# One more group of four FFN tiles with a seven-product down projection, and an end ordered by token tiles

## The chip, the cores and the metric

The kernel runs on one core of a Trainium2 chip. The metric is the device time of the core in microseconds (us). Lower is better.

## The reference

One layer of a decoder trunk over 512 tokens of width 1024, in float32. A combined input projection feeds a block-sparse attention group, an SSD (Mamba-2) group and a pooling group; their concatenation is projected and added to x. Then follows what the change touches, a SwiGLU FFN of hidden width 2816, and a final RMSNorm:

```
h = rmsnorm(x, norm_ffn)
gate, up = split(h @ w_gate_up, 2)
x = x + (silu(gate) * up) @ w_down
out = rmsnorm(x, norm_final)
```

## The kernel before

Every float32 product is made of three matmuls (`mm3`): both operands are split into a high part rounded to fp32r and a low remainder, and high x high, high x low and low x high are summed in a PSUM bank. A split costs one ScalarE copy and one VectorE subtraction (`hi_lo`).

**Tiles.** The FFN's hidden width is cut into 22 tiles of 128. For tile i, gate and up over two halves of the tokens and two halves of the width form a 2x2 by 2x2 block product, made by seven products instead of eight (`block(i, n)`, n from 1 to 7, each of 12 matmuls of 256 columns). Products 1, 6, 7 and 4 accumulate in the left half of one bank (B); after 1, 6 and 7 ScalarE copies the running sum out (`u<-psB`, line 1275). Products 2 (A) and 5, 3 (C) go to another. `block_out` makes the activation from them, with high priority.

**Weights.** Raw weights come by DMA from SP into four buffers of the tag `raw` (`r_g`, `r_u` for gate and up, `r_d`, `r_r` for the down projection), are split into the rings `w` (8 tiles) and `wx` (10), and are used. Sums of weights that the seven products need come in two ways. From tile `ADD_FROM` on, the host's array `wgs` is loaded by SP and a second part is added on the way by a DMA from POOL (`sa`, `sum_ahead`), with two VectorE additions left (lines 1001 and 1002). Tiles before it do four additions on VectorE (lines 1009 to 1012) and load the up weights whole. `sum_ahead` is first called in tile `ADD_FROM - 1` and then once for each later tile.

**Down projection.** `GROUPS` orders the tiles into groups. A group in `FAST` has four tiles and a down projection of seven products, again over two halves of the tokens, of the output columns and of the hidden rows (`down_step`, named by product 1 to 7 and half a or b; each has two token tiles of 128, three matmuls of 512 columns each). Its operands are made by `out_fast` and `split_r`, two of its weight sums come by accumulating DMA (`sar`), two by VectorE (lines 1054 and 1055). Its steps are merged into the first two tiles of the next group by the list `MERGED`, in which n0, n1 and nl are that group's first and second tile and the tile before it. Product results are added to or subtracted from `x1`, the residual, by VectorE. A group that is not in `FAST` has a plain down projection: for both column halves h, tiles k and four token tiles t, one `mm3` of 512 columns (banks `pd`).

**The end.** In the last group (18 to 21) h = 1 runs by token tile (banks `pdl`): after the four tiles' matmuls of one token tile VectorE adds the bank to x1, ScalarE squares with a running sum, `last_rstd` makes the reciprocal root (ScalarE's square root, then four small VectorE operations), and the two halves of the row are scaled, one on VectorE and one on ScalarE (`left_out`), and sent out. The last token tile is split in two parts of 256 columns (`LAST`).

**Order.** The program order is a list (`steps`) written from these tables; `advance` places the next weight split as soon as its ring has room and a clock estimate says that the data is there. A scheduler then orders the instructions of each engine by its own estimate of readiness and by priority. `tc.issue_after(x)` forces an instruction behind x. Each engine serves its instructions in the order that results.

## Time and profile before

| | |
|---|---|
| median of 3 runs | 560.72 us (559.87 to 560.85) |
| profiled execution | 560.42 us |
| its span | 558.70 us |
| TensorE busy | 98% of the span, 3464 matmuls |
| VectorE busy | 81% |
| ScalarE busy | 57% |
| DMA | 80.51 MB, 144 GB/s on average |

PE is TensorE, PEld its weight loads, DVE is VectorE, ACT ScalarE, POOL GpSimd; SPq, ACTq and POOLq are the queues that issue DMAs. A busy share is over the span. Idle time is put down to the instruction that released the engine.

### The profile page before, as it was taken

Reading aid. Unit: us, or ns where it says so; the run is one execution under the profiler, and the core shown is the slowest. Engines: PE = TensorE matmul, PEld = TensorE weight load, DVE = VectorE, ACT = ScalarE, POOL = GpSimd, SP = SyncE. Lnnn points to the kernel's source line nnn. Section 1 sums busy time; section 2 is a strip of 40 time slices with the busy share of each in tenths; the row PEclk is TensorE's granted clock in tenths of the full one; section 3 lists DMA queues with packets and bytes.
Section 4 is the critical chain, followed back from the end, with each engine's and each line's share of the span. In section 5 each row is a group of like instructions: output and inputs, shape, how many; then the busy total and the mean of one; then the engine's idle time right before and its main releaser. Section 6 shows DMA issues by size and latency. Waiting matters only on the chain.

```text
span 558.7 us, 9204 instructions
## 1 busy us (share of the span) xinstructions
PE 546.7 (98%) x3464; PEld 495.1 (89%) x3464; DVE 450.8 (81%) x832; ACT 316.3 (57%) x589; POOL 51.2 (9%) x73
## 2 busy tenths in 40 slices
PE   8999999999999999999899999999999999999995
PEld 4998998888887889998799999899999998999984
DVE  6489766898998777997768898989899797966456
ACT  6676635777678547554345555555655545434344
POOL 2020002006110001001101110101110010000000
PEclk9999999999999999999999999999999999999999
DMA  8952232423213602389736577856975575622004
GB/s 285 310 172 77 76 129 99 132 77 97 73 39 116 262 1 57 96 260 261 213 95 172 138 196 189 251 134 189 208 220 145 156 216 149 170 76 76 1 2 150
DMA packets 29312, 80.51 MB, mean 144 GB/s; under 512 B 3388, under 2 KB 5076, under 8 KB 29268
## 3 DMA queue, kind: packets, MB, share of 16 engines
q1 hardware_dynamic: 24372, 66.29, 35.4%
q0 software_dynamic: 4320, 12.58, 13.4%
q10 hardware_dynamic: 576, 1.05, 0.5%
q8 instruction: 27, 0.44, 0.3%
q14 instruction: 17, 0.14, 0.1%
HBM read 77.80 MB, written 2.11 MB: 143 GB/s over the span
## 4 chain that ended last, share of the span: by engine, by line
PE 80%; DVE 11%; DMA 4%; ACT 2%; issue 1%; SPq 1%; DVEq 0%; ACTq 0%
PE psB L201 6%; PE psB L200 6%; PE psB L199 6%; PE psA L201 5%; PE psA L200 5%; PE psA L199 5%; PE pc L199 4%; PE pc L201 4%; PE pc L200 4%; PE po L199 2%; PE po L200 2%; PE po L201 2%; PE pn L199 2%; PE pn L200 2%; PE pn L201 2%; PE dnB L199 2%
## 5 line engine op out<-in xcount | busy, mean ns | idle before, releaser
L1275 ACT COPY u<-psB 128x256 f32<-128x256 f32 x63 | 23.0, 366 | 46.9 <-PE psB L201 46.6
L169 DVE TENSOR_TENSOR wlo<-raw,whi 128x1024 fp32r<-128x1024 f32 (+4 forms) x35 | 37.2, 1065 | 12.4 <-ACT whi L168 9.2
L168 ACT ACTIVATE whi<-raw 128x1024 fp32r<-128x1024 f32 (+4 forms) x36 | 31.9, 890 | 21.9 <-PE pc L200 11.6
L199 PE MATMUL pc<-hT_hi,whi 128*128 128x512 f32 x104 | 41.7, 401 | 0.0
L201 PE MATMUL pc<-hT_hi,wlo 128*128 128x512 f32 x104 | 40.8, 392 | 0.0
L200 PE MATMUL pc<-hT_lo,whi 128*128 128x512 f32 x104 | 40.7, 391 | 0.0
L927 DVE TENSOR_TENSOR gl<-r_g,gh 128x1024 fp32r<-128x1024 f32 x22 | 26.8, 1218 | 9.5 <-ACT gh L926 9.5
L986 POOL DMA_DIRECT2D sa<-wgs x18 | 15.6, 869 | 184.9 <-DMA sa<-wgs 49.4
L926 ACT ACTIVATE gh<-r_g 128x1024 fp32r<-128x1024 f32 x22 | 23.2, 1054 | 13.7 <-DMA r_g<-wgu 7.5
L927 DVE TENSOR_TENSOR sl<-sa,sh 128x1024 fp32r<-128x1024 f32 x21 | 25.6, 1217 | 3.3 <-ACT sh L926 3.3
L926 ACT ACTIVATE sh<-r_g 128x1024 fp32r<-128x1024 f32 x18 | 19.0, 1057 | 15.8 <-PE psA L200 6.4
L199 PE MATMUL pd<-dh,aTh 128*128 128x512 f32 x64 | 24.8, 395 | 1.7 <-DVE g L1267 1.5
L199 PE MATMUL po<-whi,mixT_hi 128*128 128x512 f32 x64 | 25.5, 400 | 0.0
L926 ACT ACTIVATE sh<-sa 128x1024 fp32r<-128x1024 f32 x21 | 22.2, 1056 | 5.6 <-PE psB L200 4.2
L200 PE MATMUL po<-wlo,mixT_hi 128*128 128x512 f32 x64 | 25.0, 390 | 0.0
L201 PE MATMUL psB<-T2h,sl 128*128 128x256 f32 x84 | 24.0, 285 | 0.9 <-DVE sl L927 0.9
L200 PE MATMUL pd<-dl,aTh 128*128 128x512 f32 x64 | 24.7, 392 | 0.0
L926 ACT ACTIVATE vh<-r_u 128x512 fp32r<-128x512 f32 x21 | 13.2, 630 | 20.3 <-DMA r_u<-wgu 11.7
L927 DVE TENSOR_TENSOR sl<-r_g,sh 128x1024 fp32r<-128x1024 f32 x18 | 21.9, 1218 | 3.1 <-ACT sh L926 3.1
L199 PE MATMUL psB<-T2h,sh 128*128 128x256 f32 x84 | 23.8, 284 | 0.0
L199 PE MATMUL psB<-h_hi,gh 128*128 128x256 f32 x84 | 23.8, 284 | 0.0
L200 PE MATMUL psA<-h_lo,gh 128*128 128x256 f32 x84 | 23.8, 283 | 0.0
(393 smaller groups left out, 2026.6 us busy)
## 6 DMA issues: line engine op xcount, KB each, us to landing
r_g<-wgu SPq DMA_DIRECT2D x22, 512.0 KB, 4.3
sa<-wgs SPq DMA_DIRECT2D x18, 512.0 KB, 4.5
sa<-wgs POOLq DMA_DIRECT2D x18, 512.0 KB, 6.7
raw<-w SPq DMA_DIRECT2D x13, 512.0 KB, 3.2
r_d<-wd SPq DMA_DIRECT2D x10, 512.0 KB, 4.0
r_u<-wgu SPq DMA_DIRECT2D x18, 256.0 KB, 3.9
r_r<-wd SPq DMA_DIRECT2D x18, 256.0 KB, 3.2
raw<-wo SPq DMA_DIRECT2D x8, 512.0 KB, 3.2
```

The source lines that it names most:

```text
L168: high = nc.scalar.activation(hi[:, sl], raw[:, sl], AF.Copy)
L169: eng.tensor_tensor(lo[:, sl], raw[:, sl], hi[:, sl].bitcast(F32), ALU.subtract)
L199: nc.tensor.matmul(ps, s_hi, m_hi, start=first, stop=False, skip_group_check=chain)
L200: nc.tensor.matmul(ps, s_hi, m_lo, start=False, stop=False, skip_group_check=chain)
L201: last_mm = nc.tensor.matmul(ps, s_lo, m_hi, start=False, stop=last, skip_group_check=chain)
L926: high[name] = nc.scalar.activation(hi, src, AF.Copy).ins
L927: eng.tensor_tensor(lo, src, hi.bitcast(F32), ALU.subtract)
L986: nc.gpsimd.dma_start(t_, wgs[2 * key[0] + 1], accum_op=ALU.add)
L1275: nc.scalar.copy(u_, e["B"])
```

## The change

The fifth group becomes tiles 16 to 19 and joins `FAST`; the last group is tiles 20 and 21. The fifth group's seven products are merged into tiles 20 and 21 by a list of their own, `ENDING`. In it product 5 has banks of its own (D), and product 2's banks are left open: the last two tiles' plain down projection, the steps `k` (k, which tile or 2 for both, token tile, column half), is added onto them for token tiles 0 and 1 of the left half. Product 3 is done inside the steps k220 and k230, onto D for token tile 2 and into a new bank for token tile 3, whose x1 takes D's content by an addition of its own. From product 3 of tile 21 on, `at_end` forces TensorE's order step by step. Token tiles now finish one after the other: `half_done` squares the first half and multiplies it by the final norm's weights, `finish` does what followed the last half. `ADD_FROM` goes from 4 to 5, so tile 4 adds its weights on VectorE. The diff, cut:

```diff
-GROUPS = ((0, 4), (4, 8), (8, 12), (12, 16), (16, 18), (18, 22))
+GROUPS = ((0, 4), (4, 8), (8, 12), (12, 16), (16, 20), (20, 22))
 NA = 4
 NRAW = 4
-FAST = (1, 2, 3)
+FAST = (1, 2, 3, 4)
...
+ENDING = (
+    "n0.1 1a nl.4 n0.2 1b nl.3 2a n0.5 6a n0.6 2b n0.7 6b n1.1 n0.4 7a n1.2 7b n0.3 n1.5 4a n1.6 4b n1.7 n1.4 n1.3 5a 5b k000 k001 k100 k101 k010 k011 k110 k111 k021 k121 k031 k131 k220 k230"
+).split()
-ADD_FROM = 4
+ADD_FROM = 5
...
         def left_out(t, r, queue=nc.scalar):
-            nc.scalar.activation(x1[t][:, :512], x1[t][:, :512], AF.Copy, scale=r)
-            queue.dma_start(out[t * P : (t + 1) * P, :512], x1[t][:, :512])
+            cs = slice(0, 512) if t < 2 else slice(512, 1024)
+            nc.scalar.activation(x1[t][:, cs], x1[t][:, cs], AF.Copy, scale=r)
+            queue.dma_start(out[t * P : (t + 1) * P, cs], x1[t][:, cs])
 
         def last_rstd(t):
 
             y = tiny.tile([P, 1], F32, name=f"rsfy{t}", tag="rsy")
             v = tiny.tile([P, 1], F32, name=f"rsfv{t}", tag="rsv")
             a = tiny.tile([P, 1], F32, name=f"rsfa{t}", tag="rsa")
-            root[t] = nc.scalar.activation(y, ss[:, t, 1:2], AF.Sqrt, scale=1.0 / D, bias=ss[:, t, 0:1]).ins
-            nc.vector.scalar_tensor_tensor(v, ss[:, t, 1:2], -0.5 / D, sh[:, t : t + 1], ALU.mult, ALU.add)
+            root[t] = nc.scalar.activation(y, ss[:, t, 1:2], AF.Sqrt, bias=ss[:, t, 0:1]).ins
+            nc.vector.tensor_scalar(v, ss[:, t, 1:2], ss[:, t, 0:1], -0.5, ALU.add, ALU.mult)
...
-                for m in MERGED:
+                for m in ENDING if hi_ == FT else MERGED:
                     if m[0] == "n":
                         put((base[m[:2]], int(m[3])))
+                    elif m[0] == "k":
+                        put(("k", *map(int, m[1:])))
                     else:
                         put(("r", gi - 1, int(m[0]), "ab".index(m[1])))
-            tiles = [i for i in range(lo_, hi_) if i not in PLAIN]
+            tiles = [i for i in range(lo_, hi_) if i not in PLAIN] if hi_ < FT else []
             for i, nxt in zip(tiles, tiles[1:] + [None]):
                 put(*((i, n) for n in ((1, 2, 5, 6, 7) if i >= ADD_FROM else (1, 2, 6, 5, 7))))
-                if nxt is None and hi_ == 18:
-                    put((hi_, 1), (i, 4), (hi_, 2), (i, 3))
-                elif nxt is None:
+                if nxt is None:
 
                     tail = [] if gi in FAST else [(i, 4), (i, 3)]
...
+                    elif q[0] == "k":
+                        if q[1] > 1:
+                            want((R_RING[2], 2, split_r, GROUPS[gi - 1][0] // 2, 3))
+                        want(("w", 2, split_d, lo_ // 2, q[3]))
...
-            if gi not in FAST:
+            if gi == 0 and gi not in FAST:
...
-                mm3(ps, w_hi[:, sl], w_lo[:, sl], *moving(n, kt), new and kt == 0, kt == 3, chain=not new)
+                mm_ = mm3(ps, w_hi[:, sl], w_lo[:, sl], *moving(n, kt), new and kt == 0, kt == 3, chain=not new)
+            if (i, n) == (FT - 1, 3):
+                at_end.append(mm_)
...
+        at_end, scaled = [], []
+        def behind(*ins):
+            return tc.issue_after(*ins) if ins else nullcontext()
 
         def down_step(_, gi, n, c):
 
             kp0 = GROUPS[gi][0] // 2
             w_hi, w_lo = need(("r", kp0, n))
-            which = "B" if n in (1, 6, 7, 4) else "A"
+            ending = GROUPS[gi][1] == FT - 2
+            which = "B" if n in (1, 6, 7, 4) else "D" if ending and n == 5 else "A"
             if (gi, which) not in acc:
                 acc[gi, which] = [bank(f"dn{which}{v}_{gi}") for v in range(2)]
             ps = acc[gi, which]
             js = slice(c * 512, (c + 1) * 512)
             a_hi, a_lo = aT[n, kp0 + c]
             new = n in (1, 2, 5)
+            goes_on = ending and n == 2
             for v in range(2):
                 vs = slice(v * P, (v + 1) * P)
-                mm3(ps[v], a_hi[:, vs], a_lo[:, vs], w_hi[:, js], w_lo[:, js], new and c == 0, c == 1, chain=not new)
+                with behind(*at_end):
+                    mm_ = mm3(ps[v], a_hi[:, vs], a_lo[:, vs], w_hi[:, js], w_lo[:, js], new and c == 0, c == 1, chain=not new)
+                if at_end:
+                    at_end[0] = mm_
             if c:
                 done(R_RING[n - 1], 2)
                 ops.pop(("r", kp0, n))
@@ -1411,9 +1430,84 @@
                         x_ = x1[t0 + v][:, cs]
                         if op:
                             nc.vector.tensor_tensor(x_, x_, ps[v], ALU.subtract)
-                        else:
+                        elif not goes_on:
                             add(x_, ps[v], x_)
+                        if ending and n == 5 and v == 1:
+                            add_x1(3, 0, ps[v])
+                if ending and n == 7:
+                    gf[0] = x1p.tile([P, D], F32, name="gf", tag="gn")
+                    nc.sync.dma_start(gf[0], gfin.to_broadcast([P, D]))
             advance()
+        def sq_out(t, c):
+            return rawp.tile([P, 1024], F32, name=f"sqf{t}{c}", tag="raw")
+        def half_done(t, h):
+            cs = slice(h * 512, (h + 1) * 512)
+            sq = nc.scalar.activation(sq_out(t, 0)[:, :512], x1[t][:, cs], AF.Square, scale=D**-0.5, accum_out=ss[:, t, 0:1])
+            if t == NT - 1:
+                with tc.issue_after(sq.ins):
+                    left_out(1, rs[1])
+            nc.vector.tensor_scalar_add(ss[:, t, 0:1], ss[:, t, 0:1], EPS)
+            nc.vector.tensor_tensor(x1[t][:, cs], x1[t][:, cs], gf[0][:, cs], ALU.mult)
+        def finish(t, h):
+            with behind(*scaled):
+                r = last_rstd(t)
+            if t in (1, 3):
+                with tc.issue_after(root[t]):
+                    left_out(t - 1, rs[t - 1], nc.sync if t == NT - 1 else nc.scalar)
+            rs[t] = r
+            os_ = slice(h * 512, (h + 1) * 512)
+            scaled[:] = [nc.vector.scalar_tensor_tensor(x1[t][:, os_], x1[t][:, os_], r, gf[0][:, os_], ALU.mult, ALU.mult).ins]
+            nc.sync.dma_start(out[t * P : (t + 1) * P, os_], x1[t][:, os_])
+            if t == NT - 1:
+                left_out(t, r)
+        banks_k = {}
+        def last_step(_, j, t, h):
+            kp, gi = FT // 2 - 1, len(GROUPS) - 2
+            w_ = need(("d", kp, h))
+            ts_ = slice(t * P, (t + 1) * P)
+            work = [(aT[FT - 2 + j_][0][:, ts_], aT[FT - 2 + j_][1][:, ts_], w_, j_) for j_ in ((j,) if j < 2 else range(2))]
+            if j > 1:
+                k3 = GROUPS[gi][0] // 2
+                w3, vs = need(("r", k3, 3)), slice((t - 2) * P, (t - 1) * P)
+                work = [(aT[3, k3 + c][0][:, vs], aT[3, k3 + c][1][:, vs], w3, c) for c in range(2)] + work
+            goes_on = h == 0 and t < 3
+            for part in (slice(0, 512),) if (t, h) != (NT - 1, 0) else (slice(0, LAST), slice(LAST, 512)):
+                key = (t, h, part.start)
+                if key not in banks_k:
+                    banks_k[key] = acc[gi, "D" if t > 1 else "A"][t % 2] if goes_on else bank(f"k{t}{h}{part.start}")
+                ps = banks_k[key]
+                for n, (a_hi, a_lo, w, c) in enumerate(work):
+                    js = slice(c * 512 + part.start, c * 512 + part.stop)
+                    with behind(*at_end):
+                        mm_ = mm3(ps[:, part], a_hi, a_lo, w[0][:, js], w[1][:, js], not goes_on and j != 1 and n == 0, j > 0 and n == len(work) - 1, chain=goes_on)
+                    at_end[0] = mm_
+                if j == 0:
+                    continue
+                x_ = x1[t][:, h * 512 + part.start : h * 512 + part.stop]
+                with tc.high_priority():
+                    add_ = nc.vector.tensor_tensor(x_, ps[:, part], x_, ALU.add)
+                    if (h == 0) == (t < 2):
+                        half_done(t, h)
+                        continue
+                    more = part.stop < 512
+                    nc.scalar.activation(sq_out(t, 1 + more)[:, part], x_, AF.Square, scale=D**-0.5, accum_out=ss3 if more else ss[:, t, 1:2])
+                    if more:
+                        continue
+                    if part.start:
+                        with tc.issue_after(add_.ins):
+                            nc.vector.tensor_tensor(ss[:, t, 0:1], ss3, ss[:, t, 0:1], ALU.add)
+                    finish(t, h)
 
...
+                elif q[0] == "k":
+                    last_step(*q)
...
-            if gi in FAST:
+            if gi or gi in FAST:
...
-                    for t in range(NT):
-                        add_x1(t, h, pss[t])
-                        if gi == len(GROUPS) - 1:
-                            if t == 0:
-                                gf[0] = x1p.tile([P, D], F32, name="gf", tag="gn")
-                                nc.sync.dma_start(gf[0], gfin.to_broadcast([P, D]))
-                            square(t, h, rawp)
-                            nc.vector.tensor_scalar_mul(sh[:, t : t + 1], ss[:, t, 0:1], -0.5)
-                            nc.vector.tensor_tensor(x1[t][:, :512], x1[t][:, :512], gf[0][:, :512], ALU.mult)
...
-                        parts = (slice(0, 512),) if t < NT - 1 else (slice(0, LAST), slice(LAST, 512))
-                        for part in parts:
-                            ps = bank(f"pdl_{t}_{part.start}")
-                            for k in range(lo_, hi_):
-                                w_hi, w_lo = ops["d", k // 2, h]
-                                js = slice((k % 2) * 512 + part.start, (k % 2) * 512 + part.stop)
-                                with tc.issue_after(pd_end):
-                                    pd_end = mm3(ps[:, part], aT[k][0][:, ts_], aT[k][1][:, ts_], w_hi[:, js], w_lo[:, js], k == lo_, k == hi_ - 1)
...
```

## Rows read from the trace of the kernel before

**Rows 1.** The page: span, busy time and share of each engine.

```profile
span 558.7 us, 9204 instructions
...
PE 546.7 (98%) x3464; PEld 495.1 (89%) x3464; DVE 450.8 (81%) x832; ACT 316.3 (57%) x589; POOL 51.2 (9%) x73
```

**Rows 2.** Busy time by stretch: from and to in us, its length, busy us of PE, PEld, DVE, ACT and POOL (instructions), granted TensorE clock, DMA share, GB/s.

```profile
200.00:300.00 100.00, 97.59 (x689) 91.11 (x687) 79.55 (x133) 51.89 (x91) 8.00 (x9) 1.00 0.53 146
300.00:520.00 220.00, 220.00 (x1564) 207.31 (x1563) 192.09 (x300) 116.40 (x191) 18.35 (x21) 1.00 0.63 167
350.00:450.00 100.00, 100.00 (x708) 94.11 (x707) 92.88 (x147) 55.28 (x91) 11.38 (x13) 1.00 0.71 189
450.00:550.00 100.00, 99.74 (x657) 91.36 (x657) 71.12 (x123) 44.48 (x79) 1.73 (x2) 1.00 0.31 88
550.00:558.70 8.70, 2.02 (x17) 1.82 (x16) 4.23 (x16) 4.09 (x11) 0.00 (x0) 0.90 0.61 226
```

**Rows 3.** TensorE's timeline where it was idle (start, us, instruction, idle time before it and what ended it); the last of these rows is also the first matmul that uses tile 21.

```profile
233.40 0.38 PE L201 MATMUL psB<-T2h,sl 128*128 128x256 f32 x1 [0.47 <-DVE sl L927]
...
238.69 0.39 PE L201 MATMUL psB<-T2h,sl 128*128 128x256 f32 x1 [0.44 <-DVE sl L927]
...
269.54 0.50 PE L199 MATMUL pd<-dh,aTh 128*128 128x512 f32 x1 [1.48 <-DVE g L1267]
...
537.94 0.50 PE L199 MATMUL pd<-dh,aTh 128*128 128x512 f32 x1 [0.26 <-ACT aTh L926]
```

**Rows 4.** TensorE's timeline: the end of the first group's down projection; the last matmul of tile 21's product 7, the first of twelve wide matmuls, the first of twenty-four narrow ones (products 4 and 3), and the first wide one behind them.

```profile
279.25 0.28 PE L199 MATMUL psB<-h_hi,gh 128*128 128x256 f32 x1
...
529.03 0.28 PE L201 MATMUL psB<-T3h,sl 128*128 128x256 f32 x1
529.15 0.40 PE L199 MATMUL pd<-dh,aTh 128*128 128x512 f32 x1
...
531.90 0.28 PE L199 MATMUL psB<-T4h,vh 128*128 128x256 f32 x1
...
534.77 0.40 PE L199 MATMUL pd<-dh,aTh 128*128 128x512 f32 x1
```

**Rows 5.** VectorE's groups from 350 to 450 us: line, operation, shapes, count | busy us, mean ns | idle before.

```profile
L927 DVE TENSOR_TENSOR rl<-r_r,rh 128x1024 fp32r<-128x1024 f32 x8 | 9.7, 1218 | 4.2 <-PE psB L200 4.2
...
L927 DVE TENSOR_TENSOR a2l<-a,a2h 128x512 fp32r<-128x512 f32 x3 | 2.0, 681 | 0.0
...
L927 DVE TENSOR_TENSOR a1l<-a,a1h 128x256 fp32r<-128x256 f32 x3 | 1.3, 418 | 0.0
```

**Rows 6.** The same for ScalarE.

```profile
L926 ACT ACTIVATE rh<-r_r 128x1024 fp32r<-128x1024 f32 x8 | 8.5, 1059 | 2.5 <-DMA r_r<-wd 1.2 <-PE psA L200 1.1 <-PE dnB L201 0.2
```

**Rows 7.** Timeline of ScalarE and VectorE between tile 21's product 7 and the use of its activation.

```profile
529.40 0.37 ACT L1275 COPY u<-psB 128x256 f32<-128x256 f32 x1 [1.69 <-PE psB L201]
529.81 0.43 DVE L1267 TENSOR_TENSOR psB<-psA,u 128x256 f32<-128x256 f32 x1 [0.81 <-ACT u L1275]
...
535.86 1.28 ACT L1289 ACT_TABLE_LOAD   x1
...
537.27 0.61 ACT L926 ACTIVATE aTh<-a 128x512 fp32r<-128x512 f32 x1
...
537.92 0.69 DVE L927 TENSOR_TENSOR aTl<-a,aTh 128x512 fp32r<-128x512 f32 x1 [1.61 <-ACT aTh L926]
```

**Rows 8.** Around the wait at 269.5 us: from the chain that ended last (start, us, what), SP's timeline, VectorE's, and times from issue to landing (KB each, us): of the 225 to 300 us stretch for `sa`, of the whole run for `r_g`.

```profile
249.05 7.71 DMA r_g<-wgu
...
261.26 4.36 DMA r_u<-wgu
...
269.15 0.34 DVE g L1267
...
245.85 1.46 SPq L985 DMA_DIRECT2D sa<-wgs  x2
...
259.95 0.68 DVE L1001 TENSOR_TENSOR r_g<-sa,r_g 128x512 f32<-128x512 f32 x1
...
sa<-wgs SPq DMA_DIRECT2D x5, 512.0 KB, 5.7
sa<-wgs POOLq DMA_DIRECT2D x5, 512.0 KB, 6.7
...
r_g<-wgu SPq DMA_DIRECT2D x22, 512.0 KB, 4.3
```

**Rows 9.** VectorE's timeline at the end, and the last output's issue.

```profile
540.34 2.48 DVE L825 TENSOR_TENSOR x<-pd,x 128x512 f32<-128x512 f32 x4 [1.73 <-PE pd L201]
...
547.08 0.15 DVE L865 SCALAR_TENSOR_TENSOR rsfv<-ss,sh 128x1 f32<-128x1 f32 x1
...
548.03 0.75 DVE L1514 SCALAR_TENSOR_TENSOR x<-x,rsfy,gf 128x512 f32<-128x512 f32 x1
548.69 0.16 DVE L866 RECIPROCAL rsfy<-rsfy 128x1 f32<-128x1 f32 x1
...
552.06 0.42 DVE L1498 TENSOR_TENSOR x<-pdl,x 128x256 f32<-128x256 f32 x1 [0.49 <-PE pdl L201]
...
552.66 0.74 DVE L1514 SCALAR_TENSOR_TENSOR x<-x,rsfy,gf 128x512 f32<-128x512 f32 x1
...
554.92 0.33 SPq L1515 DMA_DIRECT2D out<-x  x1
```

More of the change, by code (lines that the diff above doesn't have):

```diff
@@ L12 @@
-from contextlib import ExitStack
+from contextlib import ExitStack, nullcontext
 import numpy as np
@@ L815, in layer @@
         ss3 = x1p.tile([P, 1], F32, name="ss3")
-        sh = x1p.tile([P, NT], F32, name="sh")
         wxp = fpool("wx", 10)
@@ L828, in square @@
             cs = slice(h * 512, (h + 1) * 512)
-            if p_ is rawp:
-                j_ = rawp.tile([P, 1024], F32, name=f"sqf{t}{h}", tag="raw")[:, :512]
-            else:
-                j_ = p_.tile([P, 512], BF16, name=f"sq{t}{h}", tag="sq", bufs=1)
+            j_ = p_.tile([P, 512], BF16, name=f"sq{t}{h}", tag="sq", bufs=1)
             nc.scalar.activation(j_, x1[t][:, cs], AF.Square, accum_out=ss[:, t, h : h + 1])
@@ L1413, in down_step @@
                             nc.vector.tensor_tensor(x_, x_, ps[v], ALU.subtract)
-                        else:
+                        elif not goes_on:
                             add(x_, ps[v], x_)
-            advance()
+                        if ending and n == 5 and v == 1:
[3 more added lines that the diff above has]
+                    nc.sync.dma_start(gf[0], gfin.to_broadcast([P, D]))
@@ new lines, in layer @@
+                pss = [bank(f"pd{gi}{h}_{t}") for t in range(NT)]
+                for kp in range(lo_ // 2, hi_ // 2):
+                    w_hi, w_lo = need(("d", kp, h))
+                    for j in range(2):
+                        k = 2 * kp + j
+                        js = slice(j * 512, (j + 1) * 512)
+                        if h == 0 and k == lo_ + 1:
+                            for q in tail:
+                                block(*q)
+                        for t in range(NT):
+                            ts_ = slice(t * P, (t + 1) * P)
+                            mm3(pss[t], aT[k][0][:, ts_], aT[k][1][:, ts_], w_hi[:, js], w_lo[:, js], k == lo_, k == hi_ - 1)
+                        advance()
+                    done("w", 2)
+                    advance()
@@ L1518, in layer @@
+                for t in range(NT):
+                    add_x1(t, h, pss[t])
+                    advance()
         fctx.close()
```

46 lines of the change are left out of this document (removed).

## The prediction

> **What bounds the kernel now.** I read the page first, then the busy time by stretch, then TensorE's waits, then its timeline. TensorE is busy 98% of the span and VectorE 81% [rows 1]. The stretches say more: from 300 us to 520 us TensorE is busy in every microsecond, at full granted clock; between 200 and 300 us and at the very end it is not [rows 2]. After 200 us it has four recorded waits, all short: 0.47 and 0.44 us near 235 us, 1.48 us near 269.5 us, 0.26 us at 537.9 us [rows 3]. So from 280 us to the last matmul near 552 us the time is the count of matmuls times their spacing. Twelve 128x512 matmuls from 529.15 to 531.90 us take 2.75 us, 0.229 us each; twenty-four 128x256 ones from 531.90 to 534.77 us take 2.87 us, 0.12 us each [rows 4]. A matmul taken out here shortens the kernel, provided its operands and banks still come in time, and the chain behind the last matmul keeps its length.
>
> The sum is made against the profiled execution: 560.42 us, a span of 558.70 and 1.72 outside it. The median of the three runs, 560.72 us, is 0.3 us above it, which is inside what a measurement of this kernel tells from no change (about 0.2%, 1.1 us).
>
> **The matmuls.** Before, tiles 16 and 17 take 2 x 2 x 4 x 3 = 48 wide matmuls for their down projection, tiles 18 to 21 take 96 (twenty-four halves of them count as twelve). After, the fifth group takes seven products x 2 halves of k x 2 token tiles x 3 = 84; product 3 is only moved, six matmuls each into the steps k220 and k230. Tiles 20 and 21 take 48. So 144 become 132: twelve fewer x 0.229 = **-2.75 us**, with the same split of the last 512 columns into two of 256.
>
> **What pays for it on VectorE and ScalarE.** The fifth group needs 9 splits (seven r, two d) where 6 d splits stood, at 1.22 us on VectorE and 1.06 on ScalarE [rows 5, 6], and two 128x1024 additions, taken at 1.22 us too (ScalarE is busy 57% of the span [rows 1]). The function `out_fast` does nine VectorE operations for a pair of tiles (two of 512 columns at 0.68 us, seven of 256 at 0.42) where `out_aT` does two: 0.68 x 2 + 0.42 x 7 = 4.3 against 1.4 us, 2.9 a pair, 5.8 for two [rows 5]. Three more 128x512 additions to x1 come to 2.0 us. That is 3.7 + 2.4 + 5.8 + 2.0 = 13.9 us more for VectorE. From 450 to 550 us it works 71.1 us of 100 [rows 2]; 85 of 97 would be 88%. From 350 to 450 us, where the same seven products of earlier groups run, it works 92.9 of 100, and TensorE waits for nothing [rows 2]. I cost it at nothing; the cover is TensorE's own work. If the cover is gone, what is late next is a weight split, and late splits cost TensorE 0.47 and 0.44 us each where they occur [rows 3].
>
> **The wait for tile 21.** Before, twelve matmuls lie between its last product and the first matmul that needs its activation. They take 534.77 to 537.94, 3.17 instead of 2.75 us, because the rounding on ScalarE (`aTh`) is behind the addition, the Silu and a table load of 1.28 us, and ends at 537.88 [rows 3, 4, 7]. After, 5a, 5b, k000 and k001 lie there, 18 matmuls or 4.12 us: until 538.9 us on the old clock, a microsecond later than the operand was ready, and the low part (ready at 538.61) is wanted at 539.35. So 3.17 - 2.75 = **-0.42 us** goes; at worst it stays (0), if a split of d or r stands ahead of this chain.
>
> **A wait that comes.** The ending list puts `n1.7 n1.4 n1.3` together, and everything for TensorE behind them is tied to the end of n1.3 by `issue_after`. Product 4 accumulates into the columns that ScalarE must first copy out after product 7 (`u<-psB`). In the trace product 7 of tile 21 issues its last matmul at 529.03, the copy starts at 529.40 and lasts 0.37, so product 4 could go at 529.8 instead of 529.15. There, twelve matmuls of the down projection lay between (529.15 to 531.90) [rows 4, 7]; after the change nothing does, since 4b stands before n1.7. That is **+0.65 us**. From below it is nothing, if the order that is finally issued puts 4b there. From above it is 1.1 us: the addition that follows the copy writes the other half of the same bank until 530.24 [rows 7], and no row shows a matmul entering the bank at that moment. The Trainium skill ("PSUM — Partial Sum Buffer", section "PSUM bank collisions raise a hardware error") says that accesses to PSUM must be kept apart by whole bank and quadrant, not by address. By that rule the wait would be 1.1 us and the sum 0.45 us higher; no run here shows which holds. Product 3 follows product 4 and by then its own bank is read out.
>
> **Tile 4.** Its sums move from two transfers (SP, then an accumulating one on POOL) to four VectorE additions of 0.68 us in place of two, and its up weights come as 512 KB instead of 256; SP and POOL lose one transfer each, and the prefetched sums behind them start one tile later. Where this lands is the 1.48 us wait: the chain there goes through tile 4's `r_g` (issued at 249.05, 7.71 us under way, against a median of 4.3 for all 22 of its kind), ScalarE, then tile 5's `r_u` (issued 261.26), ScalarE's and VectorE's queues, and only then tile 3's addition, for which TensorE waits until 269.54 [rows 3, 8]. While `r_g` was under way, two sums of 512 KB (issued from 245.85 on) and accumulating halves on POOL were too [rows 8]. Without them I take the usual 4.3 us: 3.4 earlier, less 2 x 0.68 for the two additions, about 2.0 us, more than the wait. But the raw buffer that tile 5's load waits for may come free in another order, so I take two thirds: **-1.0 us**, with -1.48 as the one bound and +1.5 (the same wait once more) as the other.
>
> **The end.** Behind the last matmul the chain is addition, square, root, four small operations, scaling, output: 552.06 to 554.92 us and the transfer [rows 9]. It has the same operations after; one small operation fewer is beside the square, which hides it. What differs is the queue ahead. From the end of 5b to the last matmul TensorE has twelve short k-steps of three matmuls (8.2 us), then k220 (2.75) and k230 (24 narrow ones, 2.88): 13.9 us. VectorE has in it tile 21's low part (0.6), three operations on D's banks (3 x 0.62, as the four additions of 2.48 us stand), seven full additions (4.3), a half one (0.34), four products with gf and their small ones (2.7), and three times four small operations and a scaling (0.85 from 547.08 on, 0.66 from 548.03 to 548.69): 14.3 us [rows 9]. That is 0.4 us too much, and the order of token tiles makes it wait for squares and roots besides. Before, the like queue also overran: the scaling of token tile 2 ran after the last addition and cost nothing, beside the square and the root [rows 9]. After, `behind(*scaled)` keeps the last root's operations behind that scaling. I take **+0.5 us**; from below 0, from above 1.9, the three operations on D's banks, which are new here, in full.
>
> **The sum.** -2.75 - 0.42 + 0.65 - 1.0 + 0.5 = -3.0: 557.4 us, 0.6% below the median. All bounds at their best give -2.75 - 0.42 - 1.48 = -4.65, 555.8 us; all at their worst -2.75 + 1.1 + 1.5 + 1.9 = +1.75, 562.2 us.
>
> **Rivals.** *No difference.* The matmuls go, but the wait at 269.5 us stays (0), the bank wait is 1.1 and the queue at the end 1.9, and tile 21's wait goes: -0.17, 560.25 us. For it: the end queue has no room by the count above. Against it: VectorE idled 1.73 us before the first addition of the end [rows 9], and three of four terms must come out high.
>
> *Slower: a late sum for tile 5.* Its two transfers now start only with tile 4's additions, which stood at 259.95 and which I put 2 us earlier, near 258. At 5.7 us to landing on SP and 6.7 on POOL [rows 8] the sum is there at about 270.4, and its split stands in ScalarE's queue, which serves in order: if tile 3's Silu, product and rounding (0.42, 0.42 and 0.61 us, the first two taken from the 256-column rows) stand behind that split (1.06), TensorE waits until about 273.9 instead of 269.5, +4.4 us, so -2.75 - 0.42 + 0.65 + 4.4 + 0.5 = +2.4, 562.8 us. It decides from 2.0 us of added wait on. For it: just such a queue made the old wait. Against it: TensorE itself needs this sum only after the first group's down projection, which ends at 279.25 [rows 4], so nothing forces that order.
>
> *VectorE becomes the bound in the ending.* If all nine splits came late by 0.45 us, as the two near 235 us [rows 3], that is +4.1: 561.5 us; from seven on the gain is gone. Against it stand the 92.9% without a wait [rows 2].
>
> *The matmuls that go were no bound* would need waits that TensorE does not show [rows 3]; I give it nothing of its own.
>
> **How the numbers follow.** The forecast 0.66, with its own range 555.8 to 559.5; no difference 0.13 (of it 0.03 below 559.6); the late sum 0.09 (0.08 above 561.8, 0.01 level); VectorE 0.12 (0.05, 0.03 and 0.04 for faster, level, slower, by how many splits are late). So faster 0.74, the same 0.14, slower 0.12. The range goes from the best bounds, 555.8, to 560.3, where the second case ends; the cases beyond leave about 0.15 out above and a little below.
>
> **What would show it.** Right: twelve fewer wide matmuls of the down projection; no wait, or a shorter one, near 269.5 us; a TensorE wait of 0.65 to 1.1 us just before the last product 4, released by the copy or by the addition; no wait at k100; the last matmul near 549 us; the last addition within 0.5 us of it. Wrong: waits on splits in the last 50 us, a wait over 3 us between 255 and 290 us, or more than 7.5 us from the last matmul to the end.

## The result and the profile after

The kernel after takes 556.01 us (median of 4 runs, 555.91 to 556.27), the kernel before beside it 560.71 us: ratio 0.992, 95% interval 0.9903 to 0.9937. It is faster by 4.7 us where 3.3 us was forecast (3.0 by the sum, which was made against the profiled execution of 560.42 us). The profiled execution took 556.10 us with a span of 554.4 us, 4.3 us less than before's 558.7.

The page, which answers [rows 1]: span, then busy time, share and instructions of each engine.

```profile
span 554.4 us, 9231 instructions
...
PE 542.5 (98%) x3452; PEld 491.0 (89%) x3452; DVE 463.4 (84%) x851; ACT 322.4 (58%) x598; POOL 53.9 (10%) x76
```

Twelve matmuls are gone, 3464 to 3452, and VectorE has 12.6 us more work (13.9 forecast for the ending; tile 4's two additions, 1.4, come on top). Busy time by stretch, columns as in [rows 2]:

```profile
200.00:300.00 100.00, 98.78 (x700) 92.12 (x700) 82.23 (x141) 52.80 (x94) 7.12 (x8) 1.00 0.51 140
300.00:520.00 220.00, 220.00 (x1583) 207.31 (x1582) 200.33 (x316) 122.41 (x201) 21.91 (x25) 1.00 0.65 173
450.00:546.00 96.00, 96.00 (x640) 88.01 (x639) 82.41 (x140) 50.51 (x90) 5.05 (x6) 1.00 0.42 115
546.00:554.40 8.40, 0.80 (x7) 0.60 (x6) 3.26 (x12) 2.72 (x8) 0.00 (x0) 0.67 0.34 125
```

From 300 us on TensorE now works without a break to the end of its matmuls, beside a VectorE that is busy 86% of the last 96 us before 546. What TensorE waited for in the whole run (waiting tile, what ended the wait; total us, times, longest):

```profile
PE ps_warm L255 <- DVE xdt L252: 1.3, 1, 1.3
PE psB L207 <- DVE sl L930: 1.2, 2, 0.7
PE ps_q L205 <- ACT hT_hi L277: 1.0, 1, 1.0
PE ps_t L672 <- ACT pr L664: 0.6, 1, 0.6
PE ps_o L500 <- DVE mixT_lo L357: 0.2, 1, 0.2
```

The waits near 269.5 and at 537.9 us [rows 3] have no successor; only the two of `sl` near 235 us remain of those behind 200 us. TensorE's timeline, as [rows 4]: the first matmul behind the first group's down projection; the end of tile 21's product 7, the first of what follows it, the first of product 4, of 5a and of k100, and the last matmul:

```profile
278.33 0.28 PE L205 MATMUL psB<-h_hi,gh 128*128 128x256 f32 x1
...
524.06 0.28 PE L207 MATMUL psB<-T3h,sl 128*128 128x256 f32 x1
524.18 0.40 PE L205 MATMUL dnB<-rh,a4h 128*128 128x512 f32 x1
...
526.97 0.28 PE L205 MATMUL psB<-T4h,vh 128*128 128x256 f32 x1
...
529.83 0.40 PE L205 MATMUL dnD<-rh,h_hi 128*128 128x512 f32 x1
...
534.01 0.40 PE L205 MATMUL dnA<-dh,aTh 128*128 128x512 f32 x1
...
546.53 0.27 PE L207 MATMUL k<-dh,aTl 128*128 128x256 f32 x1
```

The list puts product 4 (`n1.4`) straight behind product 7 (`n1.7`). The issued order does not: twelve matmuls of 4a and 4b (`dnB<-r,a4`) stand between, and product 4 waits for nothing.

To see where the time went, I cut each profiled span at three starts: A, the first matmul of the first group's down projection (`pd`); B, the first 256-column one behind that projection; C, the last matmul. Before against after, in us:

| stretch | before | after | difference |
|---|---|---|---|
| start to A | 251.26 | 251.65 | +0.39 |
| A to B | 27.99 | 26.68 | -1.31 |
| B to C | 272.49 | 268.20 | -4.29 |
| C to the end | 6.96 | 7.87 | +0.91 |
| span | 558.70 | 554.40 | -4.30 |

The forecast had nothing, -1.0, -2.75 - 0.42 + 0.65 = -2.52, and +0.5 in these four. So A to B came about as told, B to C gave 1.8 us more, and the end took 0.4 more. The experiments take these apart; the same cuts of each stand in a table behind them.

### The profile page after: what moved, and what is told of

Same layout as the page of the kernel before. It is cut to its first block, busy times and chain, and to the rows that moved or that the text cites. A ratio compares the mean times of both kernels' runs of the same rounds, so it can differ in the third digit from the quotient of the medians.

```text
span 554.4 us, 9231 instructions
## 1 busy us (share of the span) xinstructions
PE 542.5 (98%) x3452; PEld 491.0 (89%) x3452; DVE 463.4 (84%) x851; ACT 322.4 (58%) x598; POOL 53.9 (10%) x76
## 4 chain that ended last, share of the span: by engine, by line
PE 86%; DVE 9%; DMA 2%; ACT 2%; issue 1%; SPq 0%; DVEq 0%; ACTq 0%
PE psB L207 7%; PE psB L206 7%; PE psB L205 7%; PE psA L205 4%; PE psA L206 4%; PE psA L207 4%; PE pc L205 4%; PE pc L206 4%; PE pc L207 4%; PE dnB L205 3%; PE dnB L207 3%; PE dnB L206 3%; PE po L205 2%; PE po L207 2%; PE po L206 2%; PE pn L205 2%
## 5 line engine op out<-in xcount | busy, mean ns | idle before, releaser
L930 DVE TENSOR_TENSOR rl<-r_r,rh 128x1024 fp32r<-128x1024 f32 x20 | 24.3, 1217 | 5.8 <-PE psA L206 2.8
L929 ACT ACTIVATE rh<-r_r 128x1024 fp32r<-128x1024 f32 x20 | 21.2, 1060 | 11.2 <-PE psA L206 3.6
L206 PE MATMUL psB<-T2l,sh 128*128 128x256 f32 x84 | 23.7, 282 | 0.0
L207 PE MATMUL psB<-T4h,vh 128*128 128x256 f32 x84 | 23.7, 282 | 0.0
L205 PE MATMUL psA<-h_hi,gh 128*128 128x256 f32 x84 | 23.7, 282 | 0.0
L205 PE MATMUL psB<-T3h,sh 128*128 128x256 f32 x84 | 23.6, 282 | 0.0
```

What stands on the lines that cost most here:

```text
L205: nc.tensor.matmul(ps, s_hi, m_hi, start=first, stop=False, skip_group_check=chain)
L206: nc.tensor.matmul(ps, s_hi, m_lo, start=False, stop=False, skip_group_check=chain)
L207: last_mm = nc.tensor.matmul(ps, s_lo, m_hi, start=False, stop=last, skip_group_check=chain)
L929: high[name] = nc.scalar.activation(hi, src, AF.Copy).ins
L930: eng.tensor_tensor(lo, src, hi.bitcast(F32), ALU.subtract)
```

## The experiments

**One part alone: tile 4's sums on VectorE.** The kernel before with

```diff
-ADD_FROM = 4
+ADD_FROM = 5
```

> The kernel before with the start of the prefetched sums moved from tile 4 to tile 5, and nothing else. Theory (the wait near 269.5 us comes from tile 4's loads standing in line with three prefetched sums): no wait there, the first group's down projection ends 1.0 to 1.5 us earlier, 559.2 to 559.7 us against 560.7. Rival (it went in the changed kernel through something else, or comes back at another place): 560.4 to 561.0.

Measured: 559.24 us (12 runs) against 559.94, ratio 0.9981 [0.9965, 0.9997]. The wait near 269.5 us is gone and A to B takes 26.15 us instead of 27.99. What TensorE waited for there came 2.2 us earlier than in before, as the line of tile 3's addition on VectorE shows (start, us, instruction; before, then this run):

```profile
269.06 0.42 DVE L1267 TENSOR_TENSOR g<-psC,u 128x256 f32<-128x256 f32 x1
...
266.82 0.42 DVE L1267 TENSOR_TENSOR g<-psC,u 128x256 f32<-128x256 f32 x1
```

The mechanism of the -1.0 term holds (2.0 us earlier was forecast), and the interval, -0.2 to -2.0 us, has the term inside. The gain of the median, 0.7 us, is less than the 1.0 to 1.5 expected here; that the time lies in the range is owed to a faster before (559.94 us, not 560.7). The edit does not take a fixed amount off: the 19 runs of before spread from 558.51 to 563.44 us, the 12 of this kernel from 558.70 to 559.82. It is the longer times that are gone.

**One part alone: the seven products, with the old ending.** The kernel before with the new groups, the old list and the plain end:

```diff
-GROUPS = ((0, 4), (4, 8), (8, 12), (12, 16), (16, 18), (18, 22))
+GROUPS = ((0, 4), (4, 8), (8, 12), (12, 16), (16, 20), (20, 22))
-FAST = (1, 2, 3)
+FAST = (1, 2, 3, 4)
...
-                            if h == 0 and k == lo_ + 1:
+                            if h == 0 and k == (lo_ if gi == len(GROUPS) - 1 else lo_ + 1):
```

> The kernel before with the fifth group made of tiles 16 to 19 and its down projection in seven products, merged into tiles 20 and 21 by the old list; plain end as before, with the tail of tile 21 put ahead of tile 20's twelve matmuls, so that the same twelve cover it. Theory (the matmuls that go were on the path): twelve wide matmuls fewer, 2.75 us, 557.7 to 558.2 us. Rival (VectorE or the weight splits become the bound in the ending): waits on splits after 480 us, 559.5 us or more.

Measured: 563.84 us (8 runs), ratio 1.0066 [1.0037, 1.0095]: slower than before, a miss of almost 6 us. The profiled execution, the longest of the eight (567.87 us, span 565.9), shows two TensorE waits of the down projections, near 271.7 and 545.7 us:

```profile
PE pd L199 <- DVE g L1267: 2.7, 1, 2.7
PE pd L199 <- ACT aTh L926: 1.6, 1, 1.6
```

TensorE's last matmul, then VectorE's timeline behind it: the last additions, the first and the last scaling.

```profile
553.98 0.28 PE L201 MATMUL pdl<-dh,aTl 128*128 128x256 f32 x1
...
555.28 0.74 DVE L1498 TENSOR_TENSOR x<-pdl,x 128x256 f32<-128x256 f32 x2
...
557.13 0.74 DVE L1514 SCALAR_TENSOR_TENSOR x<-x,rsfy,gf 128x512 f32<-128x512 f32 x1
...
559.90 0.75 DVE L1514 SCALAR_TENSOR_TENSOR x<-x,rsfy,gf 128x512 f32<-128x512 f32 x1
```

The matmuls do get fewer: B to C is 271.01 us, 1.48 less than before although 1.6 us of wait is new in it. But C to the end is 11.92 us instead of 6.96. In the old ending all four token tiles share the last column half, which now has six matmuls a token tile instead of twelve. VectorE's additions, products with gf, small operations and scalings need the same time as ever and stand uncovered behind the last matmul: 5.0 us lost in this profile for the 2.75 saved. Another 2.74 us of its loss are the longer wait in A to B, a stretch that the edit does not touch; the profile is 4 us above the median, and what the end costs in the other runs no profile shows. The rival does not explain the loss: behind 480 us TensorE waits for tile 21's rounding alone, and for no split of a weight. So the matmul saving alone is no gain in this kernel; the ending by token tiles is what lets it through.

**One part undone: the kernel after with `ADD_FROM = 4`.**

> The changed kernel with the prefetched sums from tile 4 again. Theory: the wait of about 1.4 us near 269 us is back, 557.0 to 557.6 us against 556.0. Rival (the ending's gain does not depend on it and neither does the wait): 555.9 to 556.2.

Measured: 556.90 us (6 runs), ratio 0.9931 [0.9907, 0.9955]. Neither range was met. Its profiled execution, the shortest of the six (556.01 us), has no wait near 269.5 us. So at `ADD_FROM = 4` this wait is 1.48 us in one profile (before), 2.70 in another (the seven products above) and absent in a third. The first link of the chain differs with it: tile 4's `r_g`, issued at 249.05 us in before, landed after 7.7 us; with the seven products it took 7.2, and tile 5's `r_u` 6.0 instead of 4.4; here, issued at 249.26, it took 5.5. ScalarE's first use of it, before and here:

```profile
256.78 1.06 ACT L926 ACTIVATE gh<-r_g 128x1024 fp32r<-128x1024 f32 x1 [4.07 <-DMA r_g<-wgu]
...
254.82 1.06 ACT L929 ACTIVATE gh<-r_g 128x1024 fp32r<-128x1024 f32 x1 [1.99 <-DMA r_g<-wgu]
```

Why one load takes longer than the other is not shown. The six runs reach from 556.01 to 558.15 us; what `ADD_FROM` is worth inside the new kernel lies within this scatter and stays open.

**The places of the buffers alone.** The change removes a small tile, `sh`, and every buffer allocated behind it moves by 32 bytes: the activation ring `aT` goes from byte 125824 of a partition to 125856, from a multiple of 64 to 32 past one. The kernel after with another small tile made wider puts them back; the order of instructions on each engine stays the same:

```diff
-        ss3 = x1p.tile([P, 1], F32, name="ss3")
+        ss3 = x1p.tile([P, 16], F32, name="ss3")[:, :1]
```

> The changed kernel with a tile of 4 bytes made 64 bytes wide, so that all FFN buffers laid down after it (x1, wx, sums, aT, g, u) lie at the addresses of the kernel before, 32 bytes lower; every engine's instructions and their order are the same. In the changed kernel narrow matmuls of the FFN come every 0.1185 us instead of 0.1198, wide ones every 0.2325 instead of 0.2275. Theory (the addresses set that spacing): 0.1198 and 0.2275 come back, which by the counts behind 279 us (1536 and 372) is +2.0 - 1.9, so within 0.5 us of 556.0, mostly seen in the spacing. Rival (the spacing belongs to the chip or the run): 0.1185 and 0.2325 stay.

Measured: 556.38 us (6 runs), ratio 0.9922 [0.9897, 0.9946]. The time hardly moves, but its parts do. The mean distance between neighbouring matmuls of one size, start to start, behind B, in us:

| | 256 to 256 columns | 512 to 512 columns |
|---|---|---|
| before | 0.1197 | 0.2315 |
| after | 0.1185 | 0.2321 |
| after, old places | 0.1196 | 0.2299 |

(Before's means hold a wait; the two kernels after have one order and can be compared.) TensorE's timeline shows it singly: from k000 to the first matmul of k220 there are 36 wide matmuls, between the last two lines 15 narrow ones. First after, then with the old places:

```profile
532.61 0.40 PE L205 MATMUL dnA<-dh,aTh 128*128 128x512 f32 x1
...
541.01 0.40 PE L205 MATMUL dnD<-rh,a2h 128*128 128x512 f32 x1
...
544.52 0.28 PE L205 MATMUL k<-dh,aTh 128*128 128x256 f32 x1
...
546.29 0.28 PE L205 MATMUL k<-dh,aTh 128*128 128x256 f32 x1
```

```profile
532.73 0.39 PE L205 MATMUL dnA<-dh,aTh 128*128 128x512 f32 x1
...
540.89 0.39 PE L205 MATMUL dnD<-rh,a2h 128*128 128x512 f32 x1
...
544.32 0.28 PE L205 MATMUL k<-dh,aTh 128*128 128x256 f32 x1
...
546.12 0.28 PE L205 MATMUL k<-dh,aTh 128*128 128x256 f32 x1
```

The wide ones take 8.40 us after and 8.16 with the old places, 0.233 and 0.227 each; the narrow ones 1.77 and 1.80. Over A to B, a stretch with many wide matmuls, the 32 bytes cost 0.53 us (26.68 against 26.15). From B to C, where 1536 narrow ones gain 0.0011 us each (1.7 us) and 372 wide ones lose 0.0022 each (0.8 us), they give 269.13 - 268.20 = 0.93 us back.

**After again, the bank wait, and the root first.** The kernel after once more, as the base of three variants:

> The changed kernel once more, as the yardstick of the three below on the same chip: 555.9 to 556.6 us, narrow matmuls of the FFN every 0.1185 us and wide ones every 0.2325.

Measured: 555.93 us (6 runs), ratio 0.9932 [0.9917, 0.9947].

In the second one product 7 of tile 21 is forced behind 4b, the order in which the prediction had priced the bank wait:

```diff
+                with behind(*(four if (i, n) == (FT - 1, 7) else [])):
+                    mm_ = mm3(ps, w_hi[:, sl], w_lo[:, sl], *moving(n, kt), new and kt == 0, kt == 3, chain=not new)
...
+                if ending and (n, c, v) == (4, 1, 1):
+                    four.append(mm_)
```

> The changed kernel with product 7 of tile 21 held behind step 4b, the order in which the ending's list is written; in the changed kernel the scheduler had put 4a and 4b between product 7 and product 4. Theory (product 4 waits for ScalarE's copy out of the same columns): a wait of 0.65 us of TensorE before product 4, released by the copy, about 0.6 us longer than the changed kernel. Rival (whole banks are kept apart, so it waits for the addition into the other half too): 1.1 us, released by VectorE. Third: no wait and no difference.

Measured: 557.31 us (6 runs), ratio 0.9957 [0.9942, 0.9972], 1.38 us over the base. The timeline of the three engines: a low part on VectorE, product 7's last matmul, ScalarE's copy, VectorE's addition, product 4's first matmul.

```profile
526.22 1.22 DVE L930 TENSOR_TENSOR rl<-r_r,rh 128x1024 fp32r<-128x1024 f32 x1
526.33 0.28 PE L207 MATMUL psB<-T3h,sl 128*128 128x256 f32 x1
526.70 0.37 ACT L1282 COPY u<-psB 128x256 f32<-128x256 f32 x1 [0.65 <-PE psB L207]
527.36 0.43 DVE L1274 TENSOR_TENSOR psB<-psA,u 128x256 f32<-128x256 f32 x1
527.84 0.38 PE L205 MATMUL psB<-T4h,vh 128*128 128x256 f32 x1 [1.23 <-DVE psB L1274]
```

The copy of the columns that product 4 adds to ends at 527.07; product 4 starts only when the addition into the other half of the same bank is over, at 527.79. It follows product 7 by 1.51 us instead of 0.12. So the term, where it occurs, is 1.39 us: my upper bound of 1.1 plus a wait of the addition behind a split on VectorE. The Trainium skill's rule ("PSUM — Partial Sum Buffer", section "PSUM bank collisions raise a hardware error"), accesses guarded by bank and quadrant and not by address, agrees with the order of this trace; what the chip would do without the program's wait, no run here shows.

In the third one token tile 2's root stands ahead of the last tile's first square on ScalarE, and its small operations ahead of the last addition on VectorE:

```diff
+                    with behind(*([root_y[2]] if (t, part.start) == (NT - 1, LAST) else [])):
+                        add_ = nc.vector.tensor_tensor(x_, ps[:, part], x_, ALU.add)
...
+                    with behind(*([root[2]] if more else [])):
+                        nc.scalar.activation(sq_out(t, 1 + more)[:, part], x_, AF.Square, scale=D**-0.5, accum_out=ss3 if more else ss[:, t, 1:2])
```

> The changed kernel with token tile 2's square root ahead of the square of the last token tile's first part on ScalarE, and its small operations ahead of the last addition on VectorE. Theory (the end is 0.9 us longer because token tile 2's root operations and scaling come after the last addition, and the last root's operations behind them): the last scaling starts 0.5 to 0.7 us earlier behind the last addition, 555.3 to 555.6 us if the changed kernel is at 556.0. Rival (the last addition is delayed by as much): no difference.

Measured: 555.45 us (5 runs), ratio 0.9922 [0.9908, 0.9936], 0.48 us under the base. The intervals of the two overlap; what shows the gain is the profile, where C to the end is 7.20 us instead of 7.82. First the end of after, on VectorE (the last addition, token tile 2's scaling, the last tile's first small operation, the last scaling) and on ScalarE (the last tile's first square and token tile 2's root), as [rows 9]:

```profile
546.84 0.42 DVE L1499 TENSOR_TENSOR x<-k,x 128x256 f32<-128x256 f32 x1 [0.82 <-PE k L207]
...
548.00 0.75 DVE L1465 SCALAR_TENSOR_TENSOR x<-x,rsfy,gf 128x512 f32<-128x512 f32 x1
548.66 0.21 DVE L869 TENSOR_SCALAR rsfv<-ss 128x1 f32<-128x1 f32 x1
...
549.54 0.75 DVE L1465 SCALAR_TENSOR_TENSOR x<-x,rsfy,gf 128x512 f32<-128x512 f32 x1
...
545.88 0.42 ACT L1504 ACTIVATE sqf<-x 128x256 f32<-128x256 f32 x1
...
546.30 0.28 ACT L868 ACTIVATE rsfy<-ss 128x1 f32<-128x1 f32 x1
```

Then the variant, VectorE alone:

```profile
546.72 0.42 DVE L1500 TENSOR_TENSOR x<-k,x 128x256 f32<-128x256 f32 x1
...
547.12 0.74 DVE L1465 SCALAR_TENSOR_TENSOR x<-x,rsfy,gf 128x512 f32<-128x512 f32 x1
547.79 0.21 DVE L869 TENSOR_SCALAR rsfv<-ss 128x1 f32<-128x1 f32 x1
...
548.80 0.75 DVE L1465 SCALAR_TENSOR_TENSOR x<-x,rsfy,gf 128x512 f32<-128x512 f32 x1
```

In after the root of token tile 2 waits for a square of the last tile, so three of its four small operations and its scaling run behind the last addition, and the last root's small operations behind them: 2.70 us from addition to last scaling. With the root first the scaling runs beside the square, as it did before the change, and it is 2.08 us, before's value too (552.06 to 554.14).

**The activations alone back on multiples of 64 bytes.** The kernel after, its activation buffers, with the copies `u` beside them, which no matmul reads, moved by 96 bytes; the order of instructions is again the same:

```diff
-                    [P, 256], F32, name=f"u{n}_{i}", tag=f"u{n}", bufs={1: U1_BUFS, 6: U6_BUFS, 7: 1}[n]
-                )
+                    [P, 264 if n == 1 else 256], F32, name=f"u{n}_{i}", tag=f"u{n}", bufs={1: U1_BUFS, 6: U6_BUFS, 7: 1}[n]
+                )[:, :256]
```

> The changed kernel with only the buffers of the activations (aT, a, a1 to a7) moved by 96 bytes, so that they lie at multiples of 64 again, while x1, wx, sums and g stay 32 bytes off; the order of all instructions is the same. Theory (wide matmuls are slowed by the place of their stationary operand aT, and narrow ones gain from the place of the weights in wx): wide 0.2275 to 0.2285, narrow 0.1185, 1.5 to 2.0 us faster than the changed kernel. Rival (both spacings follow the same buffers): either both as in the kernel before, or both unchanged.

Measured: 554.73 us (5 runs), ratio 0.9913 [0.9898, 0.9929], 1.2 us under the base, less than expected. The narrow matmuls stay 0.1184 us apart, the wide ones go from 0.2321 (base) to 0.2307 and not back to 0.2299; the 36 from k000 to k220 take 8.25 us (531.42 to 539.67). In the profiles the two stretches behind A give 0.9 us; the other 0.45 lie before A, which scatters by as much. So the place of the activations, the stationary operand of the wide matmuls (and of the last 24 narrow ones), changes the wide distance. It does not set it by itself. Each wide matmul has two operands: its activation lies in the moved `aT` buffers or in buffers that no edit moves (at a multiple of 64), its weights in the ring `w` (always at a multiple of 64) or in `wx` (32 past one in after and here). Sorted by these, the mean distance from the wide matmul before, behind B, in us; d marks the cases where one operand starts at a multiple of 64 and the other 32 past one:

| weights, activation | number | after, old places | after | activations moved |
|---|---|---|---|---|
| `w`, moved buffers | 192 | 0.2302 | 0.2332 d | 0.2298 |
| `wx`, moved buffers | 38 | 0.2317 | 0.2302 | 0.2341 d |
| `w`, unmoved buffers | 46 | 0.2281 | 0.2286 | 0.2294 |
| `wx`, unmoved buffers | 44 | 0.2293 | 0.2328 d | 0.2334 d |

The cases marked d are the four slowest. Moving the activations alone helped the 192 and hurt the 38. Of the operands of the other narrow matmuls only the weights in `wx` had moved in after, and the gain is mostly there: 1044 with weights in `wx` go from 0.1196 (old places) to 0.1183 (after), 416 with weights in `w` from 0.1196 to 0.1190. No run moves the weights alone, so for the narrow ones the cause is argued and not shown.

**Both edits together.**

> The kernel after with both small edits: token tile 2's root ahead of the last tile's first square, and the activation buffers moved by 96 bytes. Theory: the two act in different places (the last 3 us, and the wide matmuls behind 279 us), so they add: -0.5 and -1.2 us against the kernel after, about 554.2 to 554.4 us, ratio near 0.990, with 2.1 us from the last addition to the last scaling and wide matmuls 0.228 us apart. Rival: the end's queue on VectorE takes back what the matmuls gain, since the last matmul comes earlier while VectorE's work does not: 554.7 us or more, and the last addition starts over 0.5 us behind the last matmul.

Measured: 554.19 us (4 runs) against 559.81, ratio 0.9901 [0.9884, 0.9917]: the two add, 1.74 us under the base, which ran on another chip, and this is the fastest version. The wide matmuls are 0.2310 us apart where 0.228 was expected. The rival falls: the last matmul starts at 545.55 us, and the end on VectorE is

```profile
545.93 0.41 DVE L1500 TENSOR_TENSOR x<-k,x 128x256 f32<-128x256 f32 x1
...
546.33 0.74 DVE L1465 SCALAR_TENSOR_TENSOR x<-x,rsfy,gf 128x512 f32<-128x512 f32 x1
...
548.00 0.75 DVE L1465 SCALAR_TENSOR_TENSOR x<-x,rsfy,gf 128x512 f32<-128x512 f32 x1
```

The cuts of the profiled executions, in us:

| kernel | to A | A to B | B to C | C to end | span |
|---|---|---|---|---|---|
| before, `ADD_FROM` 5 | 252.18 | 26.15 | 272.47 | 7.00 | 557.8 |
| before, seven products | 252.24 | 30.73 | 271.01 | 11.92 | 565.9 |
| after, `ADD_FROM` 4 | 251.38 | 26.66 | 268.30 | 7.76 | 554.1 |
| after, old places | 251.08 | 26.15 | 269.13 | 7.84 | 554.2 |
| after again | 251.60 | 26.68 | 268.20 | 7.82 | 554.3 |
| after, bank wait | 251.12 | 26.68 | 269.71 | 7.89 | 555.4 |
| after, root first | 251.53 | 26.67 | 268.20 | 7.20 | 553.6 |
| after, activations moved | 251.15 | 26.33 | 267.65 | 7.87 | 553.0 |
| after, both edits | 251.47 | 26.29 | 267.79 | 7.25 | 552.8 |

A to B and B to C of after repeat to a hundredth of a microsecond (after and after again); the time up to A differs by half a microsecond even between kernels that are the same up to there (after again 251.60, bank wait 251.12).

## Why the prediction was right, and where it was off

Direction and range held, and the mechanism of the main term. The total is off by 1.3 us, and that it came out better than forecast is in part luck: the bank wait that was counted (0.65) did not occur, and the places of the buffers, which were not thought of, gave 0.40. Two of the prediction's own signs failed: no wait stands before product 4, and from the last matmul to the end it is 7.87 us, over the 7.5 that were to show it wrong. By its terms:

- **Matmuls, -2.75, and the wait for tile 21, -0.42: right.** With the buffers in their old places B to C falls by 272.49 - 269.13 = 3.36 us, against 3.17 for the two terms. Tile 21's rounded activation is there before k100 at 534.01 us, as these lines of after show (compare [rows 7]):

```profile
532.33 0.62 ACT L929 ACTIVATE aTh<-a 128x512 fp32r<-128x512 f32 x1
532.98 0.69 DVE L930 TENSOR_TENSOR aTl<-a,aTh 128x512 fp32r<-128x512 f32 x1 [0.17 <-ACT aTh L929]
```

- **The bank wait, +0.65: did not occur.** The step that failed here was to read the issued order off the list. `issue_after` ties down only what stands behind product 3; 4a and 4b were free to move and were placed between products 7 and 4. My lower bound named this case and I did not choose it. Where the wait is forced it is 1.39 us, above my upper bound, since I let the addition start as soon as it could and did not look at what VectorE had before it.
- **Tile 4, -1.0: right in mechanism.** Tile 3's addition starts at 266.82 us with this edit alone, 2.2 us earlier (2.0 forecast), and the wait is gone. The stretch gains 1.84 us at the old places. As a median it is 0.7 us; the profile of before that the sum was made against had the wait, which comes and goes.
- **VectorE's work, at nothing: right**, 86% busy in the last 96 us and TensorE waits for no split there.
- **The end, +0.5: mis-sized, +0.91.** I had counted the queue (14.3 us of work in 13.9) and that the last root's operations stand behind token tile 2's scaling, but not that this tile's root would sit behind the last tile's first square on ScalarE and its small operations behind the last addition on VectorE. Undoing this order gives back 0.6 of the 0.9.
- **Left out: the places of the buffers.** I read the removed tile `sh` as one small operation fewer. It also moved FFN buffers by 32 bytes: -0.93 us from B to C, +0.53 from A to B.

The sum from these: A to B -1.84 and B to C -3.36 with the buffers in their old places, the end +0.91, the places +0.53 - 0.93 = -0.40, and the start +0.39 (the kernels after scatter by more, 251.08 to 251.65): -4.30, as measured.

Of the rivals, the late sum of tile 5 and VectorE as the bound show no wait. The time of the first was added up wrongly: 270.4 us and the four operations named (1.06, 0.42, 0.42 and 0.61) make 272.9 and not 273.9, so its price was 3.4 us and its total 561.8 us. The third, a queue at the end that eats the gain, is no fiction: it is what the seven products do without the new ending, and in their profile they lose 5.0 us by it.

## What to carry to other kernels

Work taken from the bounding engine in the last stretch uncovers what ran beside it: count, for each block of the end, the second engine's work against the matmuls left, and reorder the end before cutting them. Read waits off the order that is issued, not off the list in the source, and price a wait with the queue of the engine that must end it. When two versions differ in an allocation, compare the matmul distance of an unchanged stretch before giving the difference to the edit.

## What the runs showed of the hardware

The distance between back-to-back matmuls depends on where in SBUF their buffers start. With the same instruction order and a granted clock of 1.00 from 300 to 520 us, a shift of 32 bytes took narrow matmuls from 0.1196 to 0.1185 us and wide ones from 0.2299 to 0.2321. Wide ones were slowest, 0.2328 to 0.2341 us, where one operand started at a multiple of 64 bytes and the other 32 past one, against 0.2281 to 0.2317 where both started alike. The activations alone back on a multiple of 64 bytes gave 0.2307 and 0.1184, and 0.9 us of the profile behind A. The same wait, behind DMA transfers, was 1.48 us, 2.70 us or absent in the profiles of three kernels with `ADD_FROM = 4`; the load at the head of its chain took 7.7, 7.2 and 5.5 us.
